# A gather of rows: one batch's lower half loaded ahead of the indices, and stores in pairs

## The chip, the cores and the metric

One core of a Trainium2 chip runs the kernel. Times are device microseconds (us) from the run's start to its end, the median of several runs. The profile is of one execution, and its span runs from the first to the last instruction.

## The reference

```python
x = np.random.randn(32, 512, 1024).astype(np.float32)
indices = np.random.randint(0, 512, (32, 128)).astype(np.int32)

def reference(x, indices):
    result = np.zeros((32, 128, 1024), dtype=np.float32)
    for b in range(32):
        result[b] = x[b, indices[b]]
    return result
```

The draw is seeded. Each batch has 512 rows of 4096 bytes, of which 128 are picked with repeats. The output is 16.78 MB, and as many bytes would be read if each picked row were read once for each pick. The indices reach the kernel as 64-bit integers of which the lower 32 bits are used.

## The kernel before

The work is done batch by batch, 32 of them. The first `HEAD` = 5 batches are gathered whole. POOL (GpSimd) issues an indirect DMA that takes row `indices[b, p]` of x to partition p of the tile `block{b}`, and SP (SyncE) stores the tile. Batch 0 and batch 1 have their indices from columns of their own, `first` and `second`; all later ones from `idxT`, which TensorE makes by transposing `vals`, the 32 by 128 table of indices (tile `pos`).

The other 27 batches, in nine groups of `GROUP` = 3, are read without repeats. Three steps for each group find which picks are the first of their row and give these picks places in a list:

- `step0` spreads the indices over all partitions by TensorE (`bc`) and counts on DVE (VectorE) how many earlier picks are equal (`junk`, `cnt`, `lead`).
- `step1` ranks the first picks by TensorE (`rk`) and makes the matrix `pack` on DVE.
- `step2` makes by TensorE (`pos`) the list `at`, in which places left over hold an index that is out of bounds, and makes on DVE the 0/1 matrix `s` that takes listed rows to picks.

`fetch(b)` then gathers the listed rows into one of `RING` = 8 tiles u. An index out of bounds moves no row, so the tile keeps there what it had; that is why ACT (ScalarE) writes zeros into all u tiles at the start. `spread_rows(b)` multiplies `s` and u on TensorE, in float32, in two halves of 512 columns (tile `ps`, two records in the profile for each half); ACT copies each half to `block{b}`, and `store(b)` sends it. The tile u of batch b is used again for batch b + 8, whose gather is issued after the matmuls of batch b.

Order: DVE and TensorE run in the order of the program, enforced by `InOrder`. Four groups are prepared ahead (`AHEAD`); then each batch's spread is followed by the next fetch and by one of the three steps of a later group. SP's queue issues the stores in batch order, and each waits for its tile. Batches 10 to 14 (`HALVED`) are stored by two DMAs of 64 rows. Gathers go through one queue (software_dynamic), loads and stores issued by SP through another (hardware_dynamic). In the profile all operations that go through `InOrder` have the line of that helper, L24 or L21.

Of the kernel before, what the change touches and what calls it, by code (L numbers as in the profile page):

```python
# [6 lines left out]
F32 = mybir.dt.float32  # L7
F16 = mybir.dt.float16
I32 = mybir.dt.int32
ALU = mybir.AluOpType  # L10
# [18 lines left out]
def kernel(ctx, tc, x, indices, out):  # L29
# [10 lines left out]

    nc = tc.nc
    B, S, D = x.shape
    N = indices.shape[1]
    HEAD, RING, GROUP, AHEAD, FAR = 5, 8, 3, 4, 1024
    HALVED = range(10, 15)
    GROUPS = (B - HEAD) // GROUP
    assert S <= FAR and (B - HEAD) % GROUP == 0
    const = ctx.enter_context(tc.tile_pool(name="const", bufs=1))  # L50
    ring = ctx.enter_context(tc.tile_pool(name="ring", bufs=1))
    rows = ctx.enter_context(tc.tile_pool(name="rows", bufs=1))
    pick = ctx.enter_context(tc.tile_pool(name="pick", bufs=1))
    junkp = ctx.enter_context(tc.tile_pool(name="junk", bufs=4))
    PS = bass.MemoryType.PSUM
    pbc = ctx.enter_context(tc.tile_pool(name="pbc", bufs=2, space=PS))
    psm = ctx.enter_context(tc.tile_pool(name="psm", bufs=1, space=PS))
    pout = ctx.enter_context(tc.tile_pool(name="pout", bufs=4, space=PS))
    pe, dve = InOrder(tc), InOrder(tc)
    mm, v = nc.tensor.matmul, nc.vector  # L60


    first = const.tile([N, 1], indices.dtype, name="first")
    nc.sync.dma_start(out=first[:], in_=indices.rearrange("b n -> n b")[:, 0:1])  # L64
    vals = const.tile([B, N], indices.dtype, name="vals")
    nc.sync.dma_start(out=vals[:], in_=indices)
    second = const.tile([N, 1], indices.dtype, name="second")
    nc.sync.dma_start(out=second[:], in_=indices.rearrange("b n -> n b")[:, 1:2])


    diff = const.tile([N, N], I32, name="diff")
    nc.gpsimd.iota(diff[:], pattern=[[1, N]], base=0, channel_multiplier=-1)
    rank = const.tile([N, 8, 16], I32, name="rank")
    for e in range(8):
# [9 lines left out]
    zero = const.tile([N, 1], F32, name="zero")  # L84
    dve(v.memset, zero[:], 0.0)
    ident = const.tile([N, B], F16, name="ident")
    dve(v.tensor_scalar, out=ident[:], in0=diff[:, :B], scalar1=0, scalar2=None, op0=ALU.is_equal)
    below = const.tile([N, N], F16, name="below")
    dve(v.tensor_scalar, out=below[:], in0=diff[:], scalar1=0, scalar2=None, op0=ALU.is_lt)
    above = const.tile([N, N], F16, name="above")  # L90
# [3 lines left out]
    vf = const.tile([N, N], F16, name="vf")  # L94
    dve(v.memset, vf[:], 0.0)
    dve(v.tensor_copy, out=vf[:B],
        in_=vals[:].bitcast(I32).rearrange("p (n two) -> p n two", two=2)[:, :, 0])


    tr = psm.tile([N, B], F32, name="pos")  # L100
    pe(mm, tr[:], lhsT=vf[:], rhs=ident[:], start=True, stop=True)
    idxT = const.tile([N, B], I32, name="idxT")
# [3 lines left out]
    near = const.tile([N, B], F16, name="near")  # L106
    dve(v.tensor_scalar, out=near[:], in0=tr[:], scalar1=float(-FAR), scalar2=None, op0=ALU.add)

    xf = x.flatten_outer_dims()
    of = out.flatten_outer_dims()  # L110

    def gather(dst, at, b, **kw):
        nc.gpsimd.indirect_dma_start(  # L113
            out=dst[:], out_offset=None,
            in_=xf[:], in_offset=bass.IndirectOffsetOnAxis(ap=at, axis=0),
            element_offset=b * S * D, **kw)

    def store(b):
        step = N // 2 if b in HALVED else N
        for p in range(0, N, step):  # L120
            nc.sync.dma_start(out=of[b * N + p:b * N + p + step], in_=blocks[b][p:p + step])

    blocks = [rows.tile([N, D], F32, name=f"block{b}") for b in range(B)]
    for b in range(HEAD):
        alone = (first, second)[b:b + 1]
        gather(blocks[b], alone[0][:].bitcast(I32)[:, 0:1] if alone else idxT[:, b:b + 1], b)
        store(b)

    def table(name, dtype):
        return const.tile([N, B], dtype, name=name)  # L130

    cnt, lead, slot = table("cnt", F32), table("lead", F16), table("slot", F16)
    nth, at = table("nth", I32), table("at", I32)
    bcs, packs, spread = {}, {}, {}

    def of_group(g):
        return range(HEAD + g * GROUP, HEAD + (g + 1) * GROUP)

    def cols(t, g):
        return t[:, HEAD + g * GROUP:HEAD + (g + 1) * GROUP]  # L140

    def wide(t):
        return t.rearrange("p (g o) -> p g o", o=1).to_broadcast([N, GROUP, N])
# [1 line left out]
    def step0(g):  # L145

        bcs[g] = bc = pbc.tile([N, 4, N], F32, name="bc")
        for k, b in enumerate(of_group(g)):
            pe(mm, bc[:, k], lhsT=ident[:, b:b + 1].to_broadcast([N, N]), rhs=vf[:], start=True, stop=True)
        for k, b in enumerate(of_group(g)):  # L150
            junk = junkp.tile([N, N], F16, name="junk")
            dve(v.scalar_tensor_tensor, out=junk[:], in0=bc[:, k], scalar=idxF[:, b:b + 1], in1=below[:],
                op0=ALU.is_equal, op1=ALU.mult, accum_out=cnt[:, b:b + 1])
        dve(v.tensor_scalar, out=cols(lead, g), in0=cols(cnt, g), scalar1=0.0, scalar2=None, op0=ALU.is_equal)

    def step1(g):

        rk = psm.tile([N, GROUP], F32, name="rk")
        pe(mm, rk[:], lhsT=above[:], rhs=cols(lead, g), start=True, stop=True)
        dve(v.tensor_copy, out=cols(nth, g), in_=rk[:])  # L160
        dve(v.tensor_tensor, out=cols(nth, g), in0=cols(nth, g), in1=cols(shift, g), op=ALU.bitwise_xor)
        dve(v.scalar_tensor_tensor, out=cols(slot, g), in0=cols(cnt, g), scalar=256.0, in1=cols(nth, g),
            op0=ALU.mult, op1=ALU.add)
        packs[g] = pack = junkp.tile([N, GROUP, N], F16, name="pack")
        dve(v.tensor_tensor, out=pack[:], in0=turn[:].rearrange("p (o n) -> p o n", o=1).to_broadcast([N, GROUP, N]),
            in1=wide(cols(slot, g)), op=ALU.is_equal)

    def step2(g):

        pos = psm.tile([N, GROUP], F32, name="pos")  # L170
        for k, b in enumerate(of_group(g)):
            pe(mm, pos[:, k:k + 1], lhsT=packs[g][:, k], rhs=near[:, b:b + 1], start=True, stop=True)
        dve(v.tensor_scalar, out=cols(at, g), in0=pos[:], scalar1=float(FAR), scalar2=None, op0=ALU.add)
        s = pick.tile([N, GROUP, N], F32, name=f"s{g}")
        dve(v.tensor_tensor, out=s[:], in0=bcs[g][:, :GROUP], in1=wide(cols(at, g)), op=ALU.is_equal)
        for k, b in enumerate(of_group(g)):
            spread[b] = s[:, k]

    def fetch(b):
        if HEAD <= b < B:  # L180
            gather(held[(b - HEAD) % RING], at[:, b:b + 1], b, bounds_check=S - 1, oob_is_err=False)

    held = []
    for k in range(RING):
        u = ring.tile([N, D], F32, name=f"u{k}")
        nc.scalar.copy(out=u[:], in_=zero[:].to_broadcast([N, D]))  # L186
        held.append(u)

    def spread_rows(b):
        for h in range(2):  # L190
            w = slice(h * 512, (h + 1) * 512)
            ps = pout.tile([N, 512], F32, name="ps")
            pe(mm, ps[:], lhsT=spread[b], rhs=held[(b - HEAD) % RING][:, w], start=True, stop=True)
            nc.scalar.copy(out=blocks[b][:, w], in_=ps[:])  # L194
        store(b)

    step0(0)
    step0(1)
    for g in range(AHEAD):
        step1(g)  # L200
        if 0 < g < AHEAD - 1:
            step0(g + 1)
        step2(g)
        for b in of_group(g):
            if b < HEAD + RING:
                fetch(b)
    for b in range(HEAD, B):
        spread_rows(b)
        fetch(b + RING)
        g, step = divmod(b - HEAD, GROUP)  # L210
        if g + AHEAD < GROUPS:
            (step0, step1, step2)[step](g + AHEAD)


# [28 lines left out]
```

## Time and profile before

| what | value |
|---|---|
| median of 4 runs | 89.01 us (88.31 to 89.47) |
| profiled execution, its own time | 89.3 us |
| its span | 87.5 us |
| moved by DMA | 32.11 MB |
| gathers (software_dynamic) | 15.24 MB |
| stores and indices (hardware_dynamic) | 16.81 MB |
| busy: TensorE, ACT, POOL, DVE | 57.7, 40.5, 34.1, 26.3 us |

Busy time is the time in which an engine runs an instruction. The DMA row of the page gives the busy share of the 16 DMA engines in each fortieth of the span, and the row under it the GB/s. Line 227 and line 238 are those of the launch.

### The profile page before, as it was taken

The numbers are of one execution on the slowest core, as the hardware profiler recorded it, in microseconds if no ns is written. First come the engines' busy times: TensorE is split into PE (matmuls) and PEld (weight loads), VectorE is DVE, ScalarE is ACT, GpSimd is POOL, SyncE is SP. The second block draws the span as 40 slices with busy tenths as digits, with TensorE's granted clock in tenths as the row PEclk, the third lists the DMA queues.
The fourth block names the chain that finished last, engine by engine and source line by source line (L and its number), as shares of the span: only waits on it lengthen the run. The fifth ranks groups of instructions, "written<-read, shape, count | busy, mean of one in ns | idle before, by whom it ended". The sixth has DMA issues, their size and how long they took to land.

```text
span 87.5 us, 775 instructions
## 1 busy us (share of the span) xinstructions
PE 57.7 (66%) x172; PEld 23.7 (27%) x172; DVE 26.3 (30%) x127; ACT 40.5 (46%) x63; POOL 34.1 (39%) x46
## 2 busy tenths in 40 slices
PE   0301331008999999999999999788788888880000
PEld 0301110003444544434544433332222322330000
DVE  2597998300044366453564640000000000000000
ACT  6999400000336665566565565345555544442000
POOL 7678787780044456544455554444000000000000
PEclk9999999999999999999999999999999999999955
DMA  0089889999999999999999999999999999999950
GB/s 0 16 236 292 221 324 421 412 420 420 418 420 414 418 420 416 420 416 418 420 416 414 418 420 408 420 420 420 414 418 420 420 420 420 420 420 420 418 214 7
DMA packets 9637, 32.11 MB, mean 367 GB/s; under 512 B 1783, under 2 KB 1815, under 8 KB 9632
## 3 DMA queue, kind: packets, MB, share of 16 engines
q1 hardware_dynamic: 5024, 16.81, 47.3%
q0 software_dynamic: 4608, 15.24, 45.1%
q14 instruction: 4, 0.03, 0.1%
q8 instruction: 1, 0.02, 0.1%
HBM read 16.81 MB, written 16.78 MB: 384 GB/s over the span
## 4 chain that ended last, share of the span: by engine, by line
DMA 49%; PE 27%; issue 5%; POOL 5%; DVE 2%; ACT 1%; SPq 0%; POOLq 0%; DVEq 0%
DMA u<-in_x_dram,at 47%; PE ps L24 26%; POOL u L113 2%; POOL block L113 2%; DMA vals<-in_indices_dram 2%; DVE junk L24 1%; PE bc L24 1%; ACT block L194 1%; SPq L64 0%; POOLq L238 0%; DVE vf L24 0%; PE pos L21 0%; DVE idxT L24 0%; DVE lead L24 0%; PE pos L24 0%
## 5 line engine op out<-in xcount | busy, mean ns | idle before, releaser
L24 PE MATMUL ps<-u,s 128*128 128x512 f32 x108 | 54.3, 637 | 8.8 <-DMA u<-in_x_dram,at 8.7
L194 ACT COPY block<-ps 128x512 f32<-128x512 f32 x54 | 31.6, 585 | 38.0 <-PE ps L24 35.3
L113 POOL DMA_INDIRECT u<-in_x_dram,at x27 | 27.5, 1017 | 24.8 <-PE ps L24 7.5
L24 PEld LDWEIGHTS ps<-u,s 128*128 128x128 f32 x108 | 19.3, 199 | 33.3 <-ACT block L194 16.8
L24 DVE SCALAR_TENSOR_TENSOR junk<-bc,idxF,below 128x128 f16<-128x128 f32 x27 | 8.0, 347 | 12.9 <-PE bc L24 12.9
L186 ACT COPY u<-zero 128x1024 f32<-128x1024 f32 x8 | 7.7, 1040 | 0.0
L24 PE MATMUL pos<-near,pack 128*128 128x1 f16 x27 | 2.0, 168 | 4.8 <-DVE pack L24 4.8
L24 DVE TENSOR_TENSOR pack<-turn,slot 128x384 f16<-128x384 f16 x9 | 5.0, 558 | 0.3
L24 DVE TENSOR_TENSOR s<-bc,at 128x384 f32<-128x384 f32 x9 | 5.0, 558 | 0.3
L24 PEld LDWEIGHTS <-pack 128*128 128x128 f16 x27 | 1.7, 102 | 10.4 <-DVE pack L24 9.1
L24 PE MATMUL bc<-vf,ident 128*128 128x128 f16 x27 | 3.6, 267 | 1.3 <-DVE s L24 1.3
L24 PEld LDWEIGHTS <-ident 128*128 128x128 f16 x27 | 2.6, 117 | 5.8 <-issue 5.8
L113 POOL DMA_INDIRECT block<-in_x_dram,idxT x3 | 2.8, 944 | 0.9 <-issue 0.6
L24 PE MATMUL rk<-lead,above 128*128 128x3 f16 x9 | 1.5, 167 | 2.5 <-DVE at L24 1.5
L24 DVE CAST nth<-rk 128x3 int32<-128x3 f32 x9 | 1.5, 163 | 4.3 <-PE rk L24 4.3
L24 DVE TENSOR_SCALAR at<-pos 128x3 int32<-128x3 f32 x9 | 1.4, 159 | 4.0 <-PE pos L24 3.6
L21 PE MATMUL pos<-ident,vf 128*128 128x32 f16 x1 | 0.2, 209 | 3.5 <-DVE vf L24 3.5
L24 DVE DVE_READ_ACCUMULATOR junk<-bc,idxF,below 128x1 f32 x27 | 2.2, 83 | 0.0
L24 DVE TENSOR_TENSOR nth<-nth,shift 128x3 int32<-128x3 int32 x9 | 1.6, 182 | 0.4
L24 DVE TENSOR_SCALAR lead<-cnt 128x3 f16<-128x3 f32 x9 | 1.7, 184 | 0.3
L186 ACT ACT_TABLE_LOAD x1 | 1.3, 1283 | 0.7 <-PEq L227 0.7
L24 DVE SCALAR_TENSOR_TENSOR slot<-cnt,nth 128x3 f16<-128x3 f32 x9 | 1.5, 167 | 0.3
(21 smaller groups left out, 7.0 us busy)
## 6 DMA issues: line engine op xcount, KB each, us to landing
out_dram<-block SPq DMA_DIRECT2D x27, 512.0 KB, 10.0
out_dram<-block SPq DMA_DIRECT2D x10, 256.0 KB, 9.3
u<-in_x_dram,at POOLq DMA_INDIRECT x27, 12.5
block<-in_x_dram,idxT POOLq DMA_INDIRECT x3, 8.0
vals<-in_indices_dram SPq DMA_DIRECT2D x1, 32.0 KB, 2.0
first<-in_indices_dram SPq DMA_DIRECT2D x1, 1.0 KB, 1.8
second<-in_indices_dram SPq DMA_DIRECT2D x1, 1.0 KB, 1.8
block<-in_x_dram,first POOLq DMA_INDIRECT x1, 4.6
```

Source lines behind the costliest of these rows:

```text
L21: self.last = do(*args, **kw)
L24: self.last = do(*args, **kw)
L113: nc.gpsimd.indirect_dma_start(out=dst[:], out_offset=None, in_=xf[:], in_offset=bass.IndirectOffsetOnAxis(ap=at, axis=0), element_offset= ...
L186: nc.scalar.copy(out=u[:], in_=zero[:].to_broadcast([N, D]))
L194: nc.scalar.copy(out=blocks[b][:, w], in_=ps[:])
```

## The change

Batch 4 is no longer gathered whole. Its rows 0 to 255 are loaded in order into two tiles, `early0` and `early1`, by two DMAs that ACT issues ahead of its zeroing; the first of them waits for the DVE operation that makes `ident`. Picks of row 256 and above are gathered into u0 (`half_index` gives the others an index out of bounds). `half_spread` makes three 0/1 matrices: picks in rows 0 to 127, picks in rows 128 to 255, and the identity for the gathered rows. `half_rows` multiplies each with its tile, adding all three in `ps`: the two loaded parts between the first groups' steps, the gathered part in batch 4's turn of the spreading loop. The ring now begins at batch 4 and the groups, as before, at batch 5. The column `second` goes, so batch 1 takes its indices from `idxT`. Batches 12 to 19 lie in pairs in tiles of twice the size, each pair stored by one DMA of 1 MB; no batch is stored in halves.

```diff
-    HEAD, RING, GROUP, AHEAD, FAR = 5, 8, 3, 4, 1024
-    HALVED = range(10, 15)
-    GROUPS = (B - HEAD) // GROUP
+    HEAD, RING, GROUP, AHEAD, FAR = 4, 8, 3, 4, 1024
+    HALF = HEAD
+    PAIRED = range(12, 20)
+    SPARSE = HEAD + 1
+    GROUPS = (B - SPARSE) // GROUP
...
-    pe, dve = InOrder(tc), InOrder(tc)
+    pe, dve, act = InOrder(tc), InOrder(tc), InOrder(tc)
...
-    second = const.tile([N, 1], indices.dtype, name="second")
-    nc.sync.dma_start(out=second[:], in_=indices.rearrange("b n -> n b")[:, 1:2])
...
-    dve(v.tensor_scalar, out=ident[:], in0=diff[:, :B], scalar1=0, scalar2=None, op0=ALU.is_equal)
+    mark = dve(v.tensor_scalar, out=ident[:], in0=diff[:, :B], scalar1=0, scalar2=None, op0=ALU.is_equal)
...
+    early = [rows.tile([N, D], F32, name=f"early{k}") for k in range(2)]
+    for k in range(2):
+        load = act(nc.scalar.dma_start, out=early[k][:], in_=xf[HALF * S + k * N:HALF * S + (k + 1) * N])
+        if k == 0:
+            tc.add_manual_dep(load.ins, mark.ins.name, ...)
...
+    blocks = {}
+    for b in range(B):
+        if b not in PAIRED:
+            blocks[b] = rows.tile([N, D], F32, name=f"block{b}")[:]
+        elif b % 2 == 0:
+            pair = rows.tile([N, 2, D], F32, name=f"pair{b}")
+            blocks[b], blocks[b + 1] = pair[:, 0], pair[:, 1]
+            blocks[b, "pair"] = pair
     def store(b):
-        step = N // 2 if b in HALVED else N
-        for p in range(0, N, step):
-            nc.sync.dma_start(out=of[b * N + p:b * N + p + step], in_=blocks[b][p:p + step])
+        if b not in PAIRED:
+            nc.sync.dma_start(out=of[b * N:(b + 1) * N], in_=blocks[b])
+        elif b % 2:
+            nc.sync.dma_start(out=of[(b - 1) * N:(b + 1) * N].rearrange("(t p) d -> p t d", t=2),
+                              in_=blocks[b - 1, "pair"][:])
...
-        alone = (first, second)[b:b + 1]
-        gather(blocks[b], alone[0][:].bitcast(I32)[:, 0:1] if alone else idxT[:, b:b + 1], b)
+        gather(blocks[b], first[:].bitcast(I32)[:, 0:1] if b == 0 else idxT[:, b:b + 1], b)
...
-        nc.scalar.copy(out=u[:], in_=zero[:].to_broadcast([N, D]))
+        act(nc.scalar.copy, out=u[:], in_=zero[:].to_broadcast([N, D]))
...
+    def half_index():
+        c = slice(HALF, HALF + 1)
+        dve(v.tensor_scalar, out=nth[:, c], in0=idxT[:, c], scalar1=2 * N, scalar2=FAR,
+            op0=ALU.is_lt, op1=ALU.mult)
+        dve(v.tensor_tensor, out=at[:, c], in0=nth[:, c], in1=idxT[:, c], op=ALU.add)
+    def half_spread():
+        less = const.tile([N, 1], F32, name="less")
+        dve(v.tensor_copy, out=less[:], in_=diff[:, 0:1])
+        bc = pbc.tile([N, 4, N], F32, name="bc")
+        pe(mm, bc[:, 0], lhsT=ident[:, HALF:HALF + 1].to_broadcast([N, N]), rhs=vf[:], start=True, stop=True)
+        same = pick.tile([N, 3, N], F32, name="same")
+        for k in range(2):
+            dve(v.tensor_scalar, out=same[:, k], in0=bc[:, 0], scalar1=less[:], scalar2=float(k * N),
+                op0=ALU.add, op1=ALU.is_equal)
+        dve(v.tensor_scalar, out=same[:, 2], in0=diff[:], scalar1=0, scalar2=None, op0=ALU.is_equal)
+        spread[HALF] = same
+    def half_rows(h, last):
+        w = slice(h * 512, (h + 1) * 512)
+        if not last:
+            spread[HALF, h] = pout.tile([N, 512], F32, name="ps")
+        ps, same = spread[HALF, h], spread[HALF]
+        for k in ((2,) if last else (0, 1)):
+            pe(mm, ps[:], lhsT=same[:, k], rhs=(early + held[:1])[k][:, w], start=k == 0, stop=k == 2)
+        if last:
+            nc.scalar.copy(out=blocks[HALF][:, w], in_=ps[:])
     def spread_rows(b):
         for h in range(2):
+            if b == HALF:
+                half_rows(h, True)
+                continue
...
+    half_index()
+    fetch(HALF)
     step0(0)
     step0(1)
     for g in range(AHEAD):
...
+        if g == 0:
+            half_spread()
+        elif g < 3:
+            half_rows(g - 1, False)
     for b in range(HEAD, B):
         spread_rows(b)
         fetch(b + RING)
-        g, step = divmod(b - HEAD, GROUP)
-        if g + AHEAD < GROUPS:
+        g, step = divmod(b - SPARSE, GROUP)
+        if b >= SPARSE and g + AHEAD < GROUPS:
             (step0, step1, step2)[step](g + AHEAD)
```

More of the change, by code (lines that the diff above doesn't have):

```diff
@@ L45 @@
     N = indices.shape[1]
-    HEAD, RING, GROUP, AHEAD, FAR = 5, 8, 3, 4, 1024
-    HALVED = range(10, 15)
-    GROUPS = (B - HEAD) // GROUP
-    assert S <= FAR and (B - HEAD) % GROUP == 0
+    HEAD, RING, GROUP, AHEAD, FAR = 4, 8, 3, 4, 1024
[3 more added lines that the diff above has]
+    GROUPS = (B - SPARSE) // GROUP
+    assert 2 * N <= S <= FAR and (B - SPARSE) % GROUP == 0
     const = ctx.enter_context(tc.tile_pool(name="const", bufs=1))
@@ L97 @@
         in_=vals[:].bitcast(I32).rearrange("p (n two) -> p n two", two=2)[:, :, 0])
+    xf = x.flatten_outer_dims()
+    early = [rows.tile([N, D], F32, name=f"early{k}") for k in range(2)]
+    for k in range(2):
+        load = act(nc.scalar.dma_start, out=early[k][:], in_=xf[HALF * S + k * N:HALF * S + (k + 1) * N])
+        if k == 0:
+            tc.add_manual_dep(load.ins, mark.ins.name,
+                              mybir.DependencyInfo(mybir.DependencyClass.Sync, mybir.DependencyReason.DATA),
+                              reason="not beside the column of batch 0")
     tr = psm.tile([N, B], F32, name="pos")
@@ L107 @@
     dve(v.tensor_scalar, out=near[:], in0=tr[:], scalar1=float(-FAR), scalar2=None, op0=ALU.add)
-    xf = x.flatten_outer_dims()
     of = out.flatten_outer_dims()
@@ L113, in gather @@
         nc.gpsimd.indirect_dma_start(
-            out=dst[:], out_offset=None,
+            out=dst, out_offset=None,
             in_=xf[:], in_offset=bass.IndirectOffsetOnAxis(ap=at, axis=0),
             element_offset=b * S * D, **kw)
-    def store(b):
-        step = N // 2 if b in HALVED else N
-        for p in range(0, N, step):
-            nc.sync.dma_start(out=of[b * N + p:b * N + p + step], in_=blocks[b][p:p + step])
-    blocks = [rows.tile([N, D], F32, name=f"block{b}") for b in range(B)]
+    blocks = {}
[6 more added lines that the diff above has]
+            blocks[b, "pair"] = pair
+    def store(b):
+        if b not in PAIRED:
[3 more added lines that the diff above has]
+                              in_=blocks[b - 1, "pair"][:])
     for b in range(HEAD):
-        alone = (first, second)[b:b + 1]
-        gather(blocks[b], alone[0][:].bitcast(I32)[:, 0:1] if alone else idxT[:, b:b + 1], b)
+        gather(blocks[b], first[:].bitcast(I32)[:, 0:1] if b == 0 else idxT[:, b:b + 1], b)
         store(b)
@@ L136, in of_group @@
     def of_group(g):
-        return range(HEAD + g * GROUP, HEAD + (g + 1) * GROUP)
+        return range(SPARSE + g * GROUP, SPARSE + (g + 1) * GROUP)
     def cols(t, g):
-        return t[:, HEAD + g * GROUP:HEAD + (g + 1) * GROUP]
+        return t[:, SPARSE + g * GROUP:SPARSE + (g + 1) * GROUP]
     def wide(t):
@@ L180, in fetch @@
         if HEAD <= b < B:
-            gather(held[(b - HEAD) % RING], at[:, b:b + 1], b, bounds_check=S - 1, oob_is_err=False)
+            gather(held[(b - HEAD) % RING][:], at[:, b:b + 1], b, bounds_check=S - 1, oob_is_err=False)
     held = []
```

## The prediction

> **What bounds the kernel now.** I read the slices of the page first, to see which resource is full and from when.
>
> ```profile
> span 87.5 us, 775 instructions
> ...
> DMA  0089889999999999999999999999999999999950
> GB/s 0 16 236 292 221 324 421 412 420 420 418 420 414 418 420 416 420 416 418 420 416 414 418 420 408 420 420 420 414 418 420 420 420 420 420 420 420 418 214 7
> DMA packets 9637, 32.11 MB, mean 367 GB/s; under 512 B 1783, under 2 KB 1815, under 8 KB 9632
> ```
>
> A slice is 2.19 us. From the seventh slice to the last but one the rate never leaves 408 to 421 GB/s. The 32.11 MB are what counts; the other engines only have to keep transfers queued. The stretch table gives the sums and shows where the DMA engines are not full.
>
> ```profile
> 2.00:3.00 1.00, 0.00 (x0) 0.00 (x0) 0.30 (x2) 0.99 (x3) 0.64 (x4) 1.00 0.21 34
> 3.00:4.00 1.00, 0.48 (x6) 0.49 (x7) 0.45 (x4) 1.00 (x3) 0.88 (x1) 1.00 0.01 0
> 4.00:5.00 1.00, 0.37 (x4) 0.20 (x2) 0.99 (x8) 1.00 (x3) 0.81 (x1) 1.00 0.61 78
> ...
> 10.00:11.00 1.00, 0.16 (x1) 0.11 (x1) 0.93 (x7) 0.00 (x0) 0.69 (x2) 1.00 0.68 152
> ```
> ```profile
> 2.00:13.00 11.00, 2.89 (x25) 1.80 (x26) 8.83 (x48) 7.68 (x9) 8.51 (x11) 1.00 0.70 211
> 13.00:82.00 69.00, 54.84 (x147) 21.85 (x146) 17.00 (x76) 31.61 (x54) 24.25 (x25) 1.00 1.03 418
> ```
>
> The last two columns are the DMA share and GB/s. From 13 to 82 us: 418 GB/s, full. From 2 to 13 us: 211 GB/s, so 2.32 MB went where 418 GB/s would have moved 4.60; the lost 2.28 MB are 5.4 us. Almost nothing moves before 4.5 us, because the first gather waits for its indices:
>
> ```profile
> 2.77 1.11 POOL L113 DMA_INDIRECT block<-in_x_dram,first  x1 [0.36 <-DMA first<-in_indices_dram]
> 4.19 0.95 POOL L113 DMA_INDIRECT block<-in_x_dram,second  x1 [0.30 <-issue]
> ...
> 18.86 1.00 POOL L113 DMA_INDIRECT u<-in_x_dram,at  x1 [0.31 <-issue]
> 24.05 0.99 POOL L113 DMA_INDIRECT u<-in_x_dram,at  x1 [4.19 <-PE ps L24]
> ```
>
> The last of these lines is the second thing to see: at 19.86 us the ring of eight u tiles is full, and POOL issues nothing for 4.19 us until TensorE has used the first. The timeline of TensorE says why so long (start, us, then the records; one batch is four records of ps):
>
> ```profile
> 15.13 0.24 PE L24 MATMUL pos<-near,pack 128*128 128x1 f16 x3 [1.55 <-DVE pack L24]
> 19.99 3.78 PE L24 MATMUL ps<-u,s 128*128 128x512 f32 x4 [4.62 <-DMA u<-in_x_dram,at]
> ...
> 23.89 2.75 PE L24 MATMUL ps<-u,s 128*128 128x512 f32 x4
> ...
> 26.50 1.96 PE L24 MATMUL ps<-u,s 128*128 128x512 f32 x4
> ```
>
> The first batch takes 3.78 us, the second 2.75, all later ones 1.96 (1.88 from start to start), though the granted clock reads 1.00 throughout. TensorE is slow for its first 5 us of dense work.
>
> At the end the chain of waits has the last gather, issued at 60.13, landing at 76.57, and its last copy at 78.69; at 418 GB/s until 82 us the queued stores hide that. So the end moves with (bytes) / 418 plus DMA time lost.
>
> **The change, part by part.** *Bytes.* Batch 4's whole gather (128 rows of 4096 B, 0.52 MB) goes. In its place come 256 rows as they lie (1.05 MB) and a gather of the rows from 256 up; the seeded draw has 58 such indices, 0.24 MB. The total rises by 186 rows, 0.76 MB, to 32.87 MB: +1.82 us at 418 GB/s if nothing is hidden.
>
> *Hidden part.* The two loads are issued by ACT after the DVE operation that makes ident (1.10 to 1.28 us in the timeline). The first index column was issued at 0.74 and released POOL at 2.77; an issue takes 0.4 us on SP. So I put the first bytes at about 2.4 us and the second load's some 0.5 us later. 1.05 MB are 2.5 us at 418, 2.4 to 5 us, of which the shares above leave 0.6 x 0.79 + 0.99 + 0.39 = 1.9 us idle, 0.77 MB. The other 0.28 MB meet the first gathers. From 5 to 13 us 2.32 - 0.11 = 2.21 MB were moved of the 3.34 that fit, so there are 1.1 MB of room. I take the load as wholly hidden. What then remains to be moved later is 70 rows less: -0.29 MB, **-0.69 us**. Bounds: -0.69 (all hidden) and +1.82 (nothing hidden).
>
> The Trainium skill ("DMA: Bandwidth & Descriptors", Issuing engines are not separate DMA queues) says that transfers from any issuer interleave on the same 16 engines. By that alone the load would cost its full +1.82 us. The trace says that these engines stand idle then.
>
> *Indices.* The column for batch 1 (128 small descriptors) goes, so gather 1 now needs idxT, ready at 3.95 us by the timeline (3.76 + 0.19), while POOL gets to it at 4.19: 0.24 us of slack. The load's packets run beside vals, whose landing starts the chain to idxT. Bounds: 0, or vals late by one load's half, 0.6 us, less 0.24, +0.4. I take 0.
>
> *ACT.* Two issues (0.4 us each) ahead of the table load and eight copies that ended at 9.70: now 11.3. The last u is gathered into at about 17.5 us: hidden.
>
> *POOL.* Four whole gathers instead of five, then eight u gathers with batch 4 first: the last is the 12th and issues at 17.55 instead of 18.86. Its index is of group 2, below.
>
> *DVE and PE before the first spread.* Two small DVE operations for the index (2 x 0.19), one PE broadcast and four DVE operations for `same` (about 0.16 + 3 x 0.27, from the 0.27 us cadence of junk). rk of group 1 now stands behind that broadcast, which waits for s of group 0. So group 1's indices come at about 12.3 instead of 10.70; POOL wants them at 13.5. Next `half_rows` puts 2 x 2 matmuls of 128x512 between the groups: each pair is four records, 3.4 us at the slow rate (0.85 per record, 19.99 to 23.57 has four starts) or 1.8 at the fast one. The first pair runs 11.5 to 15.0; group 2's indices follow at about 17.4 (POOL wants them at 17.55); the second pair runs 16.7 to 20.1 slow, 18.5 fast; group 3's small operations take 1.6 more; batch 4's last two matmuls, again four records, run 21.7 to 25.1 slow throughout, or 20.1 to 21.9 fast. Only then are u0 free, the gather of batch 12 issued, and the store of batch 4 sent. Before, the same point was 24.05.
>
> *What covers that.* Issued by then: gathers 2.10 + 0.24 + 7 x 0.467 = 5.61 MB (0.467 is the mean of the 27 deduplicated ones: (15.24 - 2.62) / 27), the load 1.05, four stores 2.10: 8.76 MB. Moved by 13 us: 2.29 + 1.05. At 0.419 MB per us the DMA engines run dry at 13 + 5.42 / 0.419 = 25.9 us. A gather's bytes come about 1.8 us after its issue begins (2.77 to 4.6). So the issue must be at 24.1 or earlier: true with 1.5 to 2 us to spare if TensorE is fast by the second pair, just true if it is fast by batch 4's own (23.5), false if it is slow to the end. I take no gap: **0 us**. Cover gone: rival A.
>
> The Trainium skill ("TensorE: Matmul & The Clock Gate", Part 1: The HAM clock gate) says that the fast clock needs about one busy window of 3.4 us, free-running. Before, dense work from 19.99 gave the fast rate at about 25.5, later than that; the rule would have TensorE fast by 15 to 18.4 us if windows with 70% of work count, and after 25 if they must be full, since the pairs stand apart by 1.1 us of idling.
>
> *Pairs for halves.* Batches 10 to 19 were stored by ten half and five whole transfers, and now by two whole and four double ones; SP issues less often, and the bytes are the same. Rates beside the halves (35 to 44 us) are 414 to 420, the same as elsewhere, so 0; bounds ±0.1 us (2 GB/s over 20 us). A store held back for its neighbour waits one batch, 1.9 us, in a stretch where transfers land over 10 us after their issue: hidden.
>
> **Sum.** -0.69 + 0 + 0 + 0 = -0.7. Span 87.5 to 86.8; the profiled execution took 89.3, 0.3 above the median, so I apply the difference to the median: 89.01 - 0.7 = 88.3 us. Its own range, 87.9 to 88.8.
>
> **Rivals.** A, *TensorE stays slow and the DMA engines run dry* (slower). Issue at 25.2, bytes at 27.0, dry from 25.9: 1.1 us. The store follows at 25.8, and new batches come at 1.9 to 3.4 us each with nothing queued, as at the start, where rates were 205 to 315: some 0.2 to 1.4 more. Net -0.7 + 1.3 to 2.5 = +0.6 to +1.8: 89.6 to 90.8, middle 90.2. It decides from an issue of batch 12's gather past 24.1 us on. For it: 3.78 and 2.75 us in the trace. Against: the pairs themselves warm TensorE five us earlier.
>
> B, *the load is hidden only in part.* If half of it pushes the first gathers or vals back, 128 rows, 1.25 us: 89.6; a quarter, 88.9. For it: 4 to 13 us has a DMA share of 0.6 to 1.0, though few bytes. Against: 152 GB/s at 10 us.
>
> C, *the start gains more.* With a second queue busy from 2.4 us the stalls from 5 to 12 us may shrink by a third, 0.7 us: 87.6. Nothing in the trace shows that, only the room.
>
> **How the numbers follow.** Forecast 0.53, A 0.22, B 0.14, C 0.11. I predict 88.3 us; 87.3 to 90.2 holds about 8 in 10, from below C to the middle of A. About 1% (0.9 us) is what a measurement of this kernel can tell. Faster by over 1%: C and two fifths of the forecast, 0.33. Within 1%: most of the other three fifths, half of B and a little of A, 0.42. Slower: most of A, part of B, 0.25.
>
> **What would show it.** Right: 1.05 MB more moved by 13 us than 2.32 MB; gather 1 at 4.2 us; 418 GB/s without a dip from 24 to 30 us; the gather of batch 12 before 24 us. A: a dip in those slices, and batch 4's four records at 3.4 us or more. B: the landing of the first gather pushed back and less than 3 MB by 13 us. C: over 3.6 MB by then. Wrong altogether if the steady rate leaves 418 GB/s in the paired stretch.

## The result and the profile after

The changed kernel took 88.41 us (median of 33 runs) beside 88.89 us for the kernel before (54 runs). The ratio is 0.9932, with a 95% interval of 0.9912 to 0.9951: **0.6 us faster**, forecast 0.7. The size came out as forecast, but the runs below show that it has another make-up: the early load brought little, and the pairs brought the most, by something at the end of the program that the prediction did not see. The ratio sets aside executions more than 1.5% above the fastest of their kernel (9 of the 33; the medians of all differ by 0.5 us), and of the twelve runs of `e5_delay1` below it sets aside six, at 89.3 to 90.2 us, so that what is said of that kernel holds for the other six. Below, a ratio is always to the kernel before, and a difference in us is the difference of two ratios times 88.89.

The page of the changed kernel, in the lines shown of before, and the row of instruction fetches from its DMA queues:

```profile
span 86.4 us, 801 instructions
...
DMA  0798999999999999999999999999999999999970
GB/s 1 264 421 226 268 362 401 400 421 423 425 406 419 419 423 421 412 416 419 416 417 416 416 419 421 421 419 417 419 419 418 425 408 423 419 417 425 419 306 11
DMA packets 9636, 32.86 MB, mean 381 GB/s; under 512 B 1597, under 2 KB 1629, under 8 KB 9632
...
q14 instruction: 3, 0.02, 0.1%
```

The second and third slices now carry 264 and 421 GB/s instead of 16 and 236: that is the load. The fourth and fifth are still at 226 and 268. The kernel before has one more of the instruction packets:

```profile
q14 instruction: 4, 0.03, 0.1%
```

The stretches of the changed kernel (last two columns: DMA share, GB/s):

```profile
7.00:8.00 1.00, 0.00 (x0) 0.00 (x0) 0.83 (x5) 1.00 (x2) 0.70 (x2) 1.00 0.72 131
...
2.00:13.00 11.00, 3.53 (x21) 2.22 (x22) 8.01 (x45) 8.95 (x9) 7.86 (x11) 1.00 0.90 303
13.00:82.00 69.00, 57.95 (x165) 23.05 (x163) 19.12 (x85) 32.83 (x56) 24.50 (x25) 1.00 1.03 418
```

By 13 us 3.33 MB were moved instead of 2.32, and from then on the rate is the same 418 GB/s. The hole at 7 us (131 GB/s) comes from the indices. Here is the operation of DVE that waits for `vals`, before and after, and gather 1 on POOL after:

```profile
3.24 0.22 DVE L24 CAST vf<-vals 32x128 f16<-32x128 int32 x1 [0.61 <-DMA vals<-in_indices_dram]
```
```profile
3.87 0.21 DVE L24 CAST vf<-vals 32x128 f16<-32x128 int32 x1 [1.23 <-DMA vals<-in_indices_dram]
...
4.84 0.95 POOL L124 DMA_INDIRECT block<-in_x_dram,idxT  x1 [0.97 <-DVE nth L24]
```

Before, DVE had vals at 3.24 us; now at 3.87, since vals lands beside the load. Gather 1 issues at 4.84 us instead of 4.19, and those behind it are as late. In `e7_vals_act` below, where gather 1 issues at 4.26 us, the same slice has 283 GB/s.

TensorE did what the forecast took. The second pair already runs at the fast rate, and the gather of batch 12 issues at 21.90 us:

```profile
11.57 3.36 PE L24 MATMUL ps<-early,same 128*128 128x512 f32 x4
...
16.33 1.96 PE L24 MATMUL ps<-early,same 128*128 128x512 f32 x4
...
19.67 1.96 PE L24 MATMUL ps<-u,same 128*128 128x512 f32 x4
```
```profile
21.90 1.00 POOL L124 DMA_INDIRECT u<-in_x_dram,at  x1 [2.65 <-PE ps L24]
```

The last part is after the data. SyncE waits for the stores to land, drains three times and meets the other engines. In the profile EVENT_SEMAPHORE is a wait, for a store or for another engine. Here are its instructions from the last landing on (duration min/median/max in ns, then first and last start), before and after; the first wait of before, at 86.1 us, is the one that the last landing released, and that of after, at 85.46 us, stands just ahead of its lines:

```profile
L238 SPq EVENT_SEMAPHORE  x3: 17/17/28, 86.1 to 87.4; - x3
L238 SPq DRAIN  x3: 7/7/113, 86.2 to 87.0; - x3
```
```profile
L298 SPq DRAIN  x3: 7/7/7, 85.5 to 85.8; - x3
L298 SPq EVENT_SEMAPHORE  x2: 17/17/17, 85.7 to 86.3; - x2
```

From the first to the last drain it takes 0.8 us before and 0.3 after, and one drain before has 113 ns instead of 7. Of the 1.1 us between the two spans, 0.65 lie ahead of the first drain and 0.5 behind it. (The profiled execution of before was 0.4 us slower than its median and that of the changed kernel 0.3 us faster, which is all of the first figure.)

### The profile page after: what moved, and what is told of

It is laid out like the page before. It is cut to its first block, busy times and chain, and to the rows that moved or that the text cites. A ratio compares the mean times of both kernels' runs of the same rounds, so it can differ in the third digit from the quotient of the medians.

```text
span 86.4 us, 801 instructions
## 1 busy us (share of the span) xinstructions
PE 61.5 (71%) x185; PEld 25.3 (29%) x185; DVE 27.6 (32%) x133; ACT 41.8 (48%) x65; POOL 33.7 (39%) x46
## 3 DMA queue, kind: packets, MB, share of 16 engines
q10 hardware_dynamic: 288, 1.05, 3.2%
## 4 chain that ended last, share of the span: by engine, by line
DMA 40%; PE 34%; DVE 10%; issue 4%; POOL 2%; ACT 1%; SPq 0%; POOLq 0%; DVEq 0%
DMA u<-in_x_dram,at 37%; PE ps L24 31%; DMA vals<-in_indices_dram 3%; DVE pack L24 3%; POOL u L124 2%; DVE junk L24 2%; DVE nth L24 1%; PE pos L24 1%; PE bc L24 1%; DVE same L24 1%; DVE slot L24 1%; ACT block L248 1%; DVE s L24 1%; SPq L68 0%; DVE at L24 0%
## 5 line engine op out<-in xcount | busy, mean ns | idle before, releaser
L24 PE MATMUL ps<-u,s 128*128 128x512 f32 x108 | 51.8, 610 | 5.5 <-DMA u<-in_x_dram,at 4.8
L124 POOL DMA_INDIRECT u<-in_x_dram,at x28 | 28.0, 1000 | 24.5 <-DMA u<-in_x_dram,at 5.7
L248 ACT COPY block<-ps 128x512 f32<-128x512 f32 x38 | 22.3, 586 | 19.5 <-PE ps L24 18.4
L24 PEld LDWEIGHTS ps<-u,s 128*128 128x128 f32 x108 | 18.4, 190 | 29.5 <-ACT block L248 16.1
L248 ACT COPY pair<-ps 128x512 f32<-128x512 f32 x16 | 9.4, 586 | 6.1 <-PE ps L24 4.5
L238 ACT COPY block<-ps 128x512 f32<-128x512 f32 x2 | 1.2, 586 | 9.9 <-PE ps L24 9.9
L24 PE MATMUL ps<-early,same 128*128 128x512 f32 x8 | 5.3, 804 | 0.0
L24 PEld LDWEIGHTS ps<-early,same 128*128 128x128 f32 x8 | 1.9, 257 | 1.5 <-issue 1.5
```

What stands on the lines that cost most here:

```text
L24: self.last = do(*args, **kw)
L124: nc.gpsimd.indirect_dma_start(out=dst, out_offset=None, in_=xf[:], in_offset=bass.IndirectOffsetOnAxis(ap=at, axis=0), element_offset=b * ...
L238: nc.scalar.copy(out=blocks[HALF][:, w], in_=ps[:])
```

## The experiments

**One part alone.** `e1_load_only` is the changed kernel with the old stores; `e2_pairs_only` is the kernel before with the new ones.

```diff
 e1_load_only, against the changed kernel
-    PAIRED = range(12, 20)
+    HALVED = range(10, 15)      # and blocks and store() as before
 e2_pairs_only, against the kernel before
-    HALVED = range(10, 15)
+    PAIRED = range(12, 20)      # and blocks and store() of the change
```

> The early load with its half gather, stores as in the kernel before (batches 10 to 14 in halves, no pairs). Theory (the gain is 70 rows fewer to move after the start): the whole gain of the change, a ratio of 0.993 to the kernel before, 0.991 to 0.995. Rival (the pairs bring the gain): 1.000.

> The kernel before with batches 12 to 19 stored in pairs and none in halves, no early load. Theory: the queue is full in that stretch at 418 GB/s with either form, so a ratio of 1.000, within 0.002. Rival (the pairs bring the gain): 0.993.

Measured: the load alone 0.9987 (0.9946 to 1.0028), the pairs alone 0.9939 (0.9904 to 0.9973). My theory said the opposite of both, and the rival was right: the pairs bring the gain. In the stretches the pairs change nothing while data move; the profile of `e2_pairs_only`:

```profile
2.00:13.00 11.00, 2.88 (x25) 1.79 (x26) 8.74 (x48) 7.68 (x9) 8.53 (x11) 1.00 0.71 214
13.00:82.00 69.00, 54.43 (x147) 21.54 (x146) 17.02 (x76) 31.60 (x54) 24.28 (x25) 1.00 1.03 418
```

But its end is short like that of the changed kernel, and that of `e1_load_only` is long, with eight waits after the data ahead of it. First `e2_pairs_only`, then `e1_load_only`, SyncE from the last landing on:

```profile
L248 SPq DRAIN  x3: 7/7/7, 85.8 to 86.1; - x3
```
```profile
L289 SPq EVENT_SEMAPHORE  x8: 28/28/28, 85.3 to 85.7; - x8
...
L289 SPq DRAIN  x3: 7/7/114, 85.8 to 86.6; - x3
```

**Is it the pairs' transfers or SyncE's program?** With every batch stored whole there are neither pairs nor halves. SyncE's instructions, counted in each trace: 83 before and in `e1_load_only`, 70 in the changed kernel and `e2_pairs_only`, 78 here.

```diff
 e8_whole, against the kernel before
-    HALVED = range(10, 15)
+    HALVED = ()
 e10_load_whole, against e1_load_only
-    HALVED = range(10, 15)
+    HALVED = ()
```

> The kernel before with every batch stored by one DMA: no halves, no pairs, no early load. In the profile of the kernel before SyncE has 83 instructions, an instruction fetch at the very end (4 instead of 3 on q14), and 0.44 us between its last two drains; with pairs 70 instructions, no such fetch and 0.05 us. Theory E (the pairs' gain is SyncE's shorter program: the fetch at the end falls away): whole stores, about 76 instructions, gain as much if that is short enough, ratio 0.995, with 0.05 us between the drains and 3 fetches; if it is still too long, 1.000 with 0.44 us and 4 fetches. Rival T (larger transfers are better for the DMA engines): about a third of the gain, 0.998, whatever the drains show.

> The early load with its half gather, every batch stored by one DMA: no halves, no pairs. Beside e8_whole it gives the load's own share without the halves. Prediction's theory (70 rows fewer): 0.69 us faster than e8_whole, ratio 0.008 lower. Rival L (the load costs the start about what it saves, by the late indices and by what it moves beside the first gathers): within 0.2 us of e8_whole.

Measured: 0.9972 (0.9936 to 1.0008) and 0.9964 (0.9927 to 1.0002). The 0.44 us that the expectation puts between the last two drains lie between the first two, at 86.18 to 86.61 us before. Here this stall is gone, and the long drain with it:

```profile
L238 SPq DRAIN  x3: 7/7/7, 85.8 to 86.2; - x3
```

The ratio of 0.997 cannot choose between the theories by itself: five or six waits in a row after the last landing, where the pairs leave one or two, take back 0.2 to 0.3 of the 0.5 us. What settled it was putting SyncE's instructions back and leaving the pairs as they are:

```diff
 e9_sp_pad, against the changed kernel
     nc.sync.dma_start(out=vals[:], in_=indices)
+    for k in range(10):
+        nc.sync.dma_start(out=pad[k:k + 1], in_=indices[k:k + 1, 0:8])
 e12_sp_pad2: the same ten loads, the first waiting for the cast of vals
```

> The changed kernel and ten loads of 64 bytes issued by SyncE right after vals, never used, so that SyncE again has as many instructions as before the change. Stores and pairs are unchanged. Theory E (SyncE's program length): the fourth fetch and the 0.4 us between the drains come back, 0.45 us more than the changed kernel, ratio to the kernel before 0.998. Rival T (the pairs' transfers): no change against the changed kernel, 0.993. If the ten loads delay the first store, 0.1 us more in both.

> e9_sp_pad moved the early loads too: ACT issued them at 3.50 instead of 1.31 us, since their semaphores waited for the ten small loads. Here SyncE issues the ten small loads after the cast of vals (3.9 us on), and ACT's loads stay at 1.31 us. In the traces so far SyncE stalls for about 0.44 us after its 79th instruction, if it has that many (83 in the kernel before and e1_load_only, 84 in e9_sp_pad), and never with 68 to 78. Theory E: the stall is back at the end with four fetches on q14, 0.44 us, and the order of SyncE's last waits adds up to 0.4: ratio to before 0.997 to 1.003, while the rows moved by 13 us stay as in the changed kernel. Rival T (the pairs' transfers are the gain): 0.993, no stall.

`e9_sp_pad` gave 1.0131 (1.0079 to 1.0182), far more than theory E, because the small loads had taken the semaphores that ACT's loads were to use, and ACT issued these at 3.50 us; 268 GB/s from 2 to 13 us instead of 303 are 0.39 MB, 0.9 us; its end is that of the next kernel. With the loads back at 1.31 us, `e12_sp_pad2` gave 1.0032 (0.9992 to 1.0072), 0.9 us more than the changed kernel. Its end, with 84 instructions, first the waits after the last landing, then the drains:

```profile
L308 SPq EVENT_SEMAPHORE  x7: 28/28/28, 86.1 to 86.5; - x7
```
```profile
L308 SPq DRAIN  x3: 7/7/124, 87.0 to 87.4; - x3
```

For 0.42 us behind the last wait nothing runs on SyncE, and the drain after that takes 124 ns; q14 has four packets. The stall comes ahead of the first drain here and behind it before, each time after the 79th instruction. The traces give the time from the wait that the last landing released to the end of the span: 1.40 us before, 0.96 in `e2_pairs_only`, 0.90 in the changed kernel, 1.20 in `e8_whole`, 1.87 in `e1_load_only`, 1.81 in `e9_sp_pad` and `e12_sp_pad2`. So the end alone makes `e12_sp_pad2` 0.9 us longer than the changed kernel, 0.5 by the stall with its long drain and 0.4 by six more waits. That is all that was measured, and it leaves nothing for the pairs' transfers, which are all there (within the 0.4 us that the intervals can tell). For `e2_pairs_only` the end gives 0.44 of the 0.54 us measured. So theory E holds: **the pairs' gain is a stall of 0.44 us, with a drain 0.1 us longer behind it, after SyncE's 79th instruction, which a program of 78 or fewer does not reach.**

**How much of the load is hidden?** Once it is left out, once it is doubled.

```diff
 e4_no_load, against the changed kernel
-    early = [rows.tile(...)] ...      # both loads, and
-            half_rows(g - 1, False)   # their matmuls
 e3_extra_load, against the changed kernel
+    spare = [rows.tile([N, D], F32, name=f"spare{k}") for k in range(2)]
+    for k in range(2):
+        act(nc.scalar.dma_start, out=spare[k][:], in_=xf[HALF * S + (k + 2) * N:HALF * S + (k + 3) * N])
```

> The changed kernel without the two early loads and without their matmuls: batch 4 gets only its 58 gathered rows, and its picks of rows 0 to 255 are left out. 1.05 MB less to move. Theory (the load is wholly hidden): no faster than the changed kernel by more than 0.2 us, ratio to the kernel before 0.991 to 0.994. Rival (half of it is paid): 1.25 us faster than the changed kernel, ratio 0.979. A late landing of the indices beside the load would show here as well: gather 1 back at 4.2 us from 4.84.

> The changed kernel and two more loads of 0.52 MB on ACT's queue right behind the first two (rows 256 to 511 of batch 4, never used), 1.05 MB more to move. By 13 us the changed kernel moved 303 GB/s x 11 us, 1.27 MB less than 418 GB/s would. Theory (a load is free wherever the DMA engines have gaps, the lull of 6 to 12 us included): at most 0.5 us more than the changed kernel, 88.4 to 88.9 us, ratio to the kernel before 0.993 to 0.999. Rival (only the time before the first gather's bytes is free): 1.05 / 0.418 = 2.5 us more, 90.9 us, ratio 1.022.

Measured: 0.9795 (0.9737 to 0.9852) without the load, so it costs 1.2 us of its 2.5 (0.6 to 1.8 by the intervals): the rival's half. In this is what the late indices cost, since gather 1 issues at 4.17 us here. Doubled: 1.0086 (1.0056 to 1.0117), 1.4 us for the second megabyte, between theory and rival; 0.4 of that is the end again, where seven waits instead of one follow the last landing (1.26 us from there to the end of the span), so that the data are 1.0 us later. From 2 to 13 us the trace of `e4_no_load` has

```profile
2.00:13.00 11.00, 2.88 (x23) 1.79 (x23) 8.72 (x49) 7.68 (x9) 8.41 (x11) 1.00 0.74 235
```

and `e3_extra_load` has

```profile
2.00:13.00 11.00, 3.57 (x21) 2.22 (x22) 8.07 (x45) 8.94 (x9) 7.91 (x11) 1.00 0.97 343
```

Against 303: the first 1.05 MB added 68 GB/s x 11 us = 0.75 MB by 13 us, 0.3 MB or 0.7 us short; the second added 0.44, 0.6 MB or 1.5 us short. One trace tells this only roughly: kernels with the same start have 211, 214 and 230 GB/s in this stretch (before, `e2_pairs_only`, `e8_whole`) and 292 to 316 (the changed kernel, `e1_load_only`, `e10_load_whole`, `e5_delay1`, `e6_delay3`), a scatter of 0.2 to 0.3 MB, 0.5 to 0.6 us.

**What the late indices cost.** `vals` goes out on ACT's queue at 0.74 us beside `first` on SyncE's; in `e11_best` the two loads are issued by SyncE.

```diff
 e7_vals_act, against the changed kernel
-    nc.sync.dma_start(out=vals[:], in_=indices)
+    act(nc.scalar.dma_start, out=vals[:], in_=indices)
 e11_best, against e7_vals_act
-        load = act(nc.scalar.dma_start, out=early[k][:], ...)
+        load = spq(nc.sync.dma_start, out=early[k][:], ...)
```

> The changed kernel with the table of indices (vals) loaded by ACT's queue, issued at 0.74 us beside first on SP's, so that it lands before the early load's bytes. Gather 1 then issues at 4.2 us again, not 4.84. Theory A (POOL's lateness of 0.65 us is covered, since the early load fills the DMA engines until 5.6 us): within 0.2 us of the changed kernel, ratio to before 0.991 to 0.995. Rival B (the lateness is paid in full, the start being bound by how early gathers queue up): 0.65 us faster than the changed kernel, ratio 0.986. Third outcome: first lands later beside vals, and gather 0 with it, some 0.1 to 0.4 us more.

> The changed kernel with the table vals loaded by ACT's queue at 0.74 us, and the two early loads issued by SyncE right after first, so that ACT's zeroing begins about 1 us earlier than with e7_vals_act (there the fifth gather waited for it, 8.30 us instead of 7.94). Theory (the start is bound by how early the gathers queue up): as e7_vals_act or 0.1 to 0.3 us better, ratio to before 0.984 to 0.989. Rival (that gain was chance): 0.993 as the changed kernel.

Measured: 0.9882 (0.9829 to 0.9935) and 0.9850 (0.9798 to 0.9902). The first is 0.4 us better than the changed kernel, uncertain by 0.5; the second is 0.7 us better, as uncertain, and the fastest of the kernels that compute the whole result. In both gather 1 follows gather 0 after the usual 0.30 us (4.26 and 4.25 us). From 2 to 13 us they move 309 and 327 GB/s; first `e7_vals_act`, then gather 1 and the stretch of `e11_best`:

```profile
2.00:13.00 11.00, 4.52 (x22) 2.56 (x23) 8.14 (x45) 8.94 (x9) 8.44 (x11) 1.00 0.91 309
```

```profile
4.25 0.95 POOL L124 DMA_INDIRECT block<-in_x_dram,idxT  x1 [0.30 <-DVE at L24]
```
```profile
2.00:13.00 11.00, 4.52 (x22) 2.56 (x23) 8.14 (x45) 8.12 (x9) 8.45 (x11) 1.00 0.95 327
```

Beside the 303 of the changed kernel these are 0.07 and 0.26 MB, 0.2 and 0.6 us, both within the scatter of kernels with the same start. So `e7_vals_act` alone decides neither for theory A nor for rival B. With `e11_best` the gain is clear of noise, but there the loads are also issued by SyncE; if that adds nothing, the two runs together put the earlier indices at 0.6 us, uncertain by 0.4. How the gain divides between the indices and the place of the loads stays open.

**Does what is queued cover TensorE?**

```diff
 e5_delay1 and e6_delay3, against the changed kernel, ahead of batch 4's spread
+            idle = pbc.tile([N, 4, N], F32, name="bc")
+            for k in range(2):        # range(6) in e6_delay3
+                pe(mm, idle[:].rearrange("p k n -> p (k n)"), lhsT=spread[HALF][:, k % 2],
+                   rhs=early[k % 2][:, :512], start=True, stop=True)
```

> The changed kernel with two more 128x512 float32 matmuls (result unused) on TensorE just ahead of batch 4's last two: 1.8 us later there. The gather of batch 12 then issues at 21.9 + 1.8 = 23.7 us, its bytes come at 25.5. By the trace 2142 rows are issued before it and 1912 moved by 24 us, 2118 by 26, so the queues run dry at 26.2. Theory (what is queued covers TensorE up to an issue at about 24.4): no change against the changed kernel, ratio to before 0.991 to 0.995. Rival (TensorE's start is on the path): 1.8 us more, ratio 1.013.

> The same with six more matmuls: 5.4 us later. The gather of batch 12 issues at 27.3, its bytes come at 29.1, and the queues are dry from 26.2. Theory: 2.9 us of empty queues and 0.2 to 1.4 us of slow restart, 3.1 to 4.3 us more than the changed kernel, ratio to before 1.028 to 1.042. Rival (on the path from the start): 5.4 us more, 1.054. Second rival (TensorE has slack throughout, as its catching up later suggests): no change, 0.993.

Measured: 0.9943 (0.9905 to 0.9982), no change by the ratio, with the gather of batch 12 issued at 24.06 us; and 1.0319 (1.0275 to 1.0363), 3.4 us more, both as the theory had it. With `e6_delay3` this gather issues at 27.45 us, and the queues run empty where the count of issued bytes puts it:

```profile
24.00:26.00 2.00, 2.00 (x6) 0.95 (x5) 0.00 (x0) 0.00 (x0) 0.00 (x0) 1.00 1.02 414
26.00:28.00 2.00, 2.00 (x6) 0.89 (x5) 0.00 (x0) 1.17 (x2) 0.55 (x1) 1.00 0.26 104
28.00:30.00 2.00, 2.00 (x9) 0.95 (x8) 0.90 (x6) 1.17 (x2) 1.28 (x2) 1.00 0.72 236
30.00:32.00 2.00, 2.00 (x6) 0.79 (x6) 1.17 (x6) 1.33 (x3) 1.06 (x2) 1.00 0.95 246
```

Three of the four stretches are far under 418: (314 + 182 + 172) GB/s x 2 us = 1.34 MB, 3.2 us. Finer stretches put 0.84 MB of this before 28.5 us, with nothing moving from 27.5 on to there, and 0.50 MB (1.2 us) in the slow restart from 28.5 to 32 us.

## Why the prediction was right, and where it was not

*The end moves with bytes over 418 GB/s plus lost DMA time.* Right from 13 to 82 us in every kernel where the queues never ran dry (414 to 418 GB/s). Incomplete: 1.4 us of the span before lay after the last landing, and I did not look there.

*Hidden part of the load, taken as all of it, -0.69 us.* This term failed. Leaving the load out gains 1.2 us, so about half is paid. The load's net share is `e2_pairs_only` against the changed kernel, -0.06 us, `e8_whole` against `e10_load_whole`, -0.07, and `e1_load_only` by itself, -0.1. With what the end of the span costs in each taken off, the three are 0, 0 and -0.6 us, each uncertain by 0.4, which makes an estimate of -0.2 us, uncertain by 0.2, instead of the 0.69. Rival B described this part: "If half of it pushes the first gathers or vals back". Its own sign, less than 3 MB by 13 us, did not appear (3.33 MB).

*Indices, taken as 0 within 0 to +0.4 us.* Failed in the lateness: vals landed 0.62 us later, as the upper bound had it, and the slack of 0.24 was not there, since gather 1 issued 0.27 us after idxT was ready (4.57 us); it was late by 0.65 us instead of 0.4. What this cost is not shown by itself: with gather 1 on time the kernel was 0.4 and 0.7 us faster, each uncertain by 0.5, and the second with the loads on another queue as well.

*Pairs for halves, 0 within 0.1 us.* Failed: -0.5 us, by the stall at the end. The reading of the rates was right, since the pairs do not change them. The step counted that SyncE "issues less often" and gave it no price.

*No gap behind TensorE, 0 us.* Right: the second pair ran fast, 1.4 us after 3.36 us of matmuls at the slow rate (the first of the two cases weighed for the clock), and the issue came at 21.9 us. The two delays agree with the deciding point of 24.1 us: an issue at 24.06 costs nothing by the ratio, one at 27.45 costs 3.4 us. Rival A did not happen.

*ACT, POOL.* Right: the zeroing ended at 11.2 us and cost nothing.

So the total of -0.7 was right by luck: two errors of about half a microsecond cancel. The forecast with the best chance came true in its number, and B in its mechanism.

*The rules weighed.* The Trainium skill ("DMA: Bandwidth & Descriptors", Issuing engines are not separate DMA queues) has all transfers interleave on the same 16 engines. Read as the prediction read it, the load would cost all of its bytes; the runs say half. For the stall at the end it has a rule that may bear on it ("Runtime: NRT & Kernel Launch", Instruction fetch mechanics): the sequencer fetches its next block while it runs the present one, and crossing a block's end is "mostly hidden". Whether the stall is such a crossing is not shown; if it is, it was not hidden here, 0.42 to 0.44 us each time.

## What to carry to other kernels

Read the end of the span too: subtract the last landing from the span and look at what each queue does there, because half a microsecond sat behind the data and depended on how many instructions SyncE had. A transfer put into an idle stretch need not be free: half of this one was paid, and the small load of indices beside it landed 0.62 us later. Sending the indices first and on another queue, with the loads behind, made the fastest kernel. When a change has two parts, run each alone even if the sum came out as forecast.

## What the runs showed of the hardware that I had not expected

- SyncE stood still for 0.42 to 0.44 us after its 79th instruction in all four kernels that have 83 or 84, and in none of the ten with 68 to 78. Each of the four has a fourth packet on q14 within its span, 0.6 us after SyncE goes on. In the two kernels with 78 the traces have this packet 1.1 us after the span's end, and in those with 68 to 72 not at all. The packet is recorded after the stall, so whether the fetch causes it is not settled, only that the two go together.
- Each wait of SyncE for a store that has already landed takes 0.06 us. Eight in a row, when the store that lands last is the first to be waited for, took 0.5 us more in `e1_load_only` than the one wait of the changed kernel.
- After the queues had run dry, the rate was 201 to 352 GB/s from 28.5 to 32 us in `e6_delay3`, with the DMA engines 0.8 to 1.1 busy from 29 us on, and 414 after that. At the start of the kernel before it was 205 to 315 (6 to 12 us). Why the DMA engines are slow there stays open.
